# Windowed attention in steps of two heads: fixed TensorE order, scores on 64 rows a head, one division in the gate

## The chip, the cores and the metric

One Trainium2 chip, one NeuronCore of it. The number is device time in microseconds (us) of the whole program, the median of the runs. Float32 data; the large products run in float32r (operands rounded, one pass of TensorE), each operand split into a rounded part and an exact rest, and three of the four part products are added up.

## The reference

Two layers over 2048 latent tokens of width 1024 (a grid of 32 rows of 64) and 256 context tokens. Layer 0 is attention with 16 heads of 64: a latent query reads a clamped window of 8 x 16 grid positions, with a learned bias, and all 256 context keys in one softmax; context queries read the context keys. Layer 1 is a gated linear recurrence; it is not touched.

```python
s_loc = einsum('bjqhd,bkjwhd->bhjqkw', q_r, k_band) * scale + bias   # -inf outside the window
s_ctx = einsum('bjqhd,bmhd->bhjqm', q_r, k_ctx) * scale
p = softmax(concatenate([s_loc, s_ctx], -1))
o = p_loc @ v_band + p_ctx @ v_ctx
x = x + gate * ((o * silu(z)) @ w_out)                               # q, k, v, z = split(h @ w_in)
```

## The kernel before

The kernel is written in a tile framework: pools hold rotating buffers, and a scheduler, which places each instruction by its own estimate of times, sets the order of the instructions on every engine, unless `after` (L570) ties one behind another.

Layer 0 runs in three stages. The input projection writes q, k, v and z = silu(gate) to HBM (`split_out` L253, `gate_out`); the attention reads them head pair by head pair; the output projection follows. q and k are stored as two tensors each, the rounded part and the rest (`qh`, `ql`, `kh`, `kl`).

The attention (L479 on) loops over 8 pairs of heads (`hp`), and in each over 4 row groups of 8 grid rows (`g`, 512 queries) and the context queries. A row group has 4 column bands (`j`) of 128 queries, so a pair has 16 latent steps of two heads and 2 context steps. Row groups 1 and 2 read 512 window keys, 0 and 3 read 384; all read 256 context keys, so a row of scores has 768 or 640 columns. For each band and head (`a`):

- Scores (L596, L599, L615). The stationary operand is `q`, with the rounded part of a head on partitions 0 to 63 and its rest on 64 to 127; the keys stand twice, on both halves (`pair_tile` L450), so one product over 128 rows adds the products of both parts of q with `kh`, and a second one with `kl`.
- Softmax (L494 to L499). One VectorE operation adds the bias table to the scores and takes the row's minimum (the scores have their sign turned), ScalarE takes the exponential and the sum, VectorE takes the reciprocal and multiplies the row by it.
- Transposes (`turn`, L509), in pieces of 128 keys, into a bank of PSUM, copied to SBUF by ScalarE or, each sixth time, by VectorE (L513, L515).
- Weighted values (`weighted`, L522): per 128 keys one product for each head, the two heads on the two column halves of the array. Each float32 product stands as two records in the trace. The context keys are weighted for two bands at once.

At the end of a row group `gate_store` (L553) multiplies by z and stores. The bias tables come by DMA into rotating buffers (`load_table` L426: tables `tabe`, `tabi`), whose last 256 columns and masked corners GpSimd fills each time. `o_ps` has one buffer, score tiles `s` two.

Of the kernel before, what the change touches and what calls it, by code (L numbers as in the profile page):

```python
# [25 lines left out]
# scores are kept with their sign turned  # L26
# [13 lines left out]
TPS = 3  # L40
EV = "aaaaav"
TEB = 6
PB = 4
PCB = 3
# column bands whose context keys are weighted together
JB = 2
# [7 lines left out]
class Core:  # L54
# [33 lines left out]
    def ada_lanes(self, layer, g, conds, pool):  # L88
        """columns g * 512 .. + 512 of the parameters: each lane sums its rows."""
# [12 lines left out]
    def ada_sum(self, lanes, pool, psum, tag, prev):  # L102
        """TensorE sums the lanes, behind prev."""
# [22 lines left out]
    def ada_start(self, pool, psum, tag, tag2):  # L126
        """shift and scale of layer 0 from whole rows of weights: shift by lanes, scale on TensorE."""
# [49 lines left out]

    def norms(self, xts, pool, small, tag="junk"):
        """1 / rms of the rows of each tile, one column each."""
# [36 lines left out]
    def layer0_in(self):  # L216
        nc, tc, I, S = self.nc, self.tc, self.I, self.S
        with ExitStack() as st:
# [34 lines left out]
            def split_out(cg, p, t0, n, dst_h, dst_l, keys):  # L253
                oh = wk.tile([P, 512], F32R, name="oh", tag="oh")
                ol = wk.tile([P, 512], F32R, name="ol", tag="ol")
                ohv, olv, pv = oh[:, :n], ol[:, :n], p[:, :n]
                if not keys and n == 512:
                    ohv, olv = (custom(t, [[-16, 8], [P, 4], [1, 16]], 7 * 16) for t in (oh, ol))
                    pv = p.rearrange("p (r j c) -> p r j c", r=8, j=4)
                if keys:  # L260
                    nc.scalar.mul(out=ohv, in_=pv, mul=KSCALE)
                    nc.vector.scalar_tensor_tensor(olv, pv, KSCALE, ohv.bitcast(F32), ALU.mult, ALU.subtract)
                else:
                    nc.scalar.copy(out=ohv, in_=pv)
                    nc.vector.tensor_sub(olv, pv, ohv.bitcast(F32))  # L265
                r = slice(cg * P, (cg + 1) * P)
                nc.sync.dma_start(out=dst_h[r, t0:t0 + n], in_=oh[:, :n].bitcast(F32))
                nc.sync.dma_start(out=dst_l[r, t0:t0 + n], in_=ol[:, :n].bitcast(F32))

            def gate_out(cg, p, t0, n):  # L270
                sg = wk.tile([P, 512], F32, name="sg", tag="oh")
                nc.scalar.activation(sg[:, :n], p[:, :n], AF.Sigmoid)
                z = wk.tile([P, 512], F32, name="zo", tag="ol")
                nc.vector.tensor_mul(z[:, :n], p[:, :n], sg[:, :n])
                nc.sync.dma_start(out=S["z"][cg * P:(cg + 1) * P, t0:t0 + n], in_=z[:, :n])

            def q_out(pr):
                return lambda p, t0, n: split_out(pr, p, t0, n, S["qh"], S["ql"], False)

            def k_out(pr):  # L280
                return lambda p, t0, n: split_out(pr, p, t0, n, S["kh"], S["kl"], True)
# [144 lines left out]
    def load_table(self, t, head, col, g):  # L426
        """minus the bias (or a large number outside the window) for the queries of row group g,
        whose rows stand last to first."""
        nc, S = self.nc, self.S
        nk = ROWG[g][1] * 32  # L430
# [7 lines left out]
        nc.gpsimd.memset(t[:, nk:nk + CTX], 0.0)  # L438
        if g in (1, 2):
            part("ei", 0, 8, 0, 0, nr)  # L440
        elif g == 0:
            part("ei", 0, 4, 4, 0, nr)
            nc.gpsimd.memset(t[64:128, 256:nk], NEG)
            part("ef", 4, 8, 4, 0, 8)
        else:
            nc.gpsimd.memset(t[0:64, 0:128], NEG)
# [4 lines left out]
    def pair_tile(self, p, up, dn, hp, t0, n, tag, **kw):  # L451
        t = p.tile([P, 2, n], F32R, name=tag, tag=tag, **kw)
        for part, name in ((t[0:64], up), (t[64:128], dn)):
            src = self.S[name][hp * P:(hp + 1) * P, t0:t0 + n].rearrange("(a d) t -> d a t", a=2)
            self.nc.sync.dma_start(out=part.bitcast(F32), in_=src)
        return t

    def key_block(self, p, hp, i, **kw):
        r0, nr = KBLOCKS[i]
        return [self.pair_tile(p, nm, nm, hp, r0 * 64, nr * 64, f"{nm}{nr}", **kw) for nm in ("kh", "kl")]  # L460

    def first_loads(self, hp, qp, kp, cxp):
        L = {"k": {}, "q": {}, "t": {}}
        L["q"][0] = self.pair_tile(qp, "qh", "ql", hp, 0, 512, "q")
        L["k"][0] = self.key_block(kp, hp, 0)
        L["kc"] = [self.pair_tile(cxp, nm, nm, hp, SEQ, CTX, "c" + nm) for nm in ("kh", "kl")]
        return L

    def attention_ahead(self):
        """what the first scores of the first pair of heads read."""  # L470
        self.sa = ExitStack()
        ap = self.sa.enter_context(self.tc.tile_pool(name="a0", bufs=1, reuse_waits="tile", side="right"))
        self.ahead = L = self.first_loads(0, ap, ap, ap)
        for col in (0, 1):
            for a in range(2):
                t = L["t"][0, a, col] = ap.tile([P, 640], F32, name=f"tab{a}{col}")
                self.load_table(t, a, col, 0)

    def attention(self):  # L479
        nc, tc, S = self.nc, self.tc, self.S  # L480
        with ExitStack() as st:
            def pool(name, bufs, **kw):
                return st.enter_context(tc.tile_pool(name=name, bufs=bufs, reuse_waits="tile", **kw))
            vp, kp, qp, cxp = pool("av", 2), pool("ak", 2), pool("aq", 2), pool("ac", 2)
            ti, te = pool("ai", 6), pool("ae", TEB)
            wk, sm = pool("aw", PB), pool("as", 8)
            ps_s, ps_t, ps_o = pool("aps", 2, space=PSUM), pool("apt", TPS, space=PSUM), pool("apo", 4 - TPS, space=PSUM)

            self.nt = 1

            def softmax(sview, table, n):
                p = wk.tile([P, 768], F32, name="p", tag="p")
                nm = sm.tile([P, 1], F32, name="nm", tag="nm")
                nc.vector.tensor_tensor_reduce(p[:, :n], sview, table, 1.0, 3.0e38, ALU.add, ALU.min, nm)  # L494
                sums = sm.tile([P, 1], F32, name="sums", tag="sums")
# [728 lines left out]
```

## Time and profile before

| | |
|---|---|
| median of 3 runs | 3480.48 us (3478.44 to 3486.43) |
| profiled execution, span from first to last instruction | 3477.0 us |
| TensorE busy | 3333.7 us, 96% |
| VectorE, ScalarE, GpSimd busy | 1985.4, 1261.6, 759.9 us |
| attention, first score to last weighted value | about 891 to 1607 us |

The profiled execution has no time of its own beside its span; the runs' median stands 3.5 us above it, which is what lies around the first and the last instruction. A matmul's record covers its whole passage through the array, and records overlap, so the busy share of TensorE says little: what an instruction costs is read from the distance between the starts of neighbours. PEld is the loading of the stationary operand, which runs beside matmuls.

### The profile page before, as it was taken

What the parts mean: (1) busy time and instruction counts of PE and PEld (TensorE: products, weight loads), DVE (VectorE), ACT (ScalarE), POOL (GpSimd) and SP (SyncE); (2) the same over time, 40 slices, a digit from 0 to 9 for tenths busy, and PEclk for the clock granted to TensorE, in tenths of its full rate; (3) what the DMA queues carried; (4) which work ended last, traced back from release to release, by engine and by line L of the source; (5) the groups of instructions that cost most, each with busy time, mean ns of one, the idle gap of its engine ahead of it and who ended that gap; (6) DMA issues with size and microseconds to landing.
All of it is one profiled execution on the core that took longest, in us unless ns stands there. A gap on an engine that the chain in (4) does not pass through costs nothing. (4 is left out here: it accounts for less than half of the span.)

```text
span 3477.0 us, 57414 instructions
## 1 busy us (share of the span) xinstructions
PE 3333.7 (96%) x22276; PEld 2727.7 (78%) x22276; DVE 1985.4 (57%) x4315; ACT 1261.6 (36%) x2688; POOL 759.9 (22%) x787
## 2 busy tenths in 40 slices
PE   7999999999889999999999999999899999999898
PEld 5778989989667777777888888888778777887687
DVE  7674111111457666675744555555775677777876
ACT  4311110010456666664312333333443344444521
POOL 2210110010012111112322222222342222232321
PEclk9999999999989999999999999999999999999999
DMA  6665232233777778763341111111232333332542
GB/s 234 178 198 186 82 105 77 75 106 112 168 191 180 182 174 189 172 163 99 133 142 43 58 47 55 55 56 55 94 100 78 104 114 115 116 116 98 179 145 106
DMA packets 259880, 424.46 MB, mean 122 GB/s; under 512 B 34956, under 2 KB 138124, under 8 KB 259608
## 3 DMA queue, kind: packets, MB, share of 16 engines
q1 hardware_dynamic: 244824, 372.54, 37.6%
q0 software_dynamic: 14784, 48.25, 3.6%
q8 instruction: 176, 2.88, 0.4%
q14 instruction: 96, 0.79, 0.1%
HBM read 295.22 MB, written 126.96 MB: 121 GB/s over the span
## 5 line engine op out<-in xcount | busy, mean ns | idle before, releaser
L210 PE MATMUL g_ps<-h1h,g_wh 128*128 128x512 f32 x1280 | 517.1, 404 | 5.2 <-DVE qt L984 2.6
L212 PE MATMUL g_ps<-h1h,g_wl 128*128 128x512 f32 x1280 | 516.8, 404 | 0.0
L211 PE MATMUL g_ps<-h1l,g_wh 128*128 128x512 f32 x1280 | 515.3, 403 | 0.0
L210 PE MATMUL mm<-hi,wh 128*128 128x512 f32 (+1 forms) x960 | 351.1, 372 | 5.1 <-DVE ol L265 3.5
L212 PE MATMUL mm<-hi,wl 128*128 128x512 f32 (+1 forms) x960 | 353.8, 370 | 1.8 <-POOL wl L70 1.8
L211 PE MATMUL mm<-lo,wh 128*128 128x512 f32 (+1 forms) x960 | 355.3, 371 | 0.2
L210 PEld LDWEIGHTS g_ps<-h1h,g_wh 128*128 128x128 f32 x1280 | 241.9, 189 | 61.2 <-DVE qt L984 2.9
L212 PEld LDWEIGHTS g_ps<-h1h,g_wl 128*128 128x128 f32 x1280 | 241.8, 189 | 56.0
L211 PEld LDWEIGHTS g_ps<-h1l,g_wh 128*128 128x128 f32 x1280 | 241.7, 189 | 54.0
L496 ACT ACTIVATE p<-p,nm 128x768 f32<-128x768 f32 (+2 forms) x288 | 243.2, 845 | 90.5 <-DVE nm L494 87.0
L70 POOL TENSOR_TENSOR g_wl<-g_raw,g_wh 128x1024 fp32r<-128x1024 f32 x86 | 210.1, 2444 | 292.8 <-ACT g_wh L67 279.9
L509 PE MATMUL tps<-ident,p 128*128 128x128 f32 x1472 | 249.5, 288 | 2.2 <-ACT pc L513 2.0
L818 DVE COPY_PREDICATED pm<-masks,lv 128x256 f32<-128x256 int32 x192 | 85.7, 447 | 271.7 <-PE lv L804 271.5
L509 PEld LDWEIGHTS tps<-ident,p 128*128 128x128 f32 x1472 | 167.0, 144 | 66.8 <-issue 56.7
L210 PEld LDWEIGHTS mm<-hi,wh 128*128 128x128 f32 x960 | 180.2, 189 | 39.4 <-DVE ol L265 4.8
L212 PEld LDWEIGHTS mm<-hi,wl 128*128 128x128 f32 x960 | 181.4, 189 | 33.5 <-POOL wl L70 2.7
L211 PEld LDWEIGHTS mm<-lo,wh 128*128 128x128 f32 x960 | 181.5, 189 | 32.5 <-issue 1.7
L522 PE MATMUL o_ps<-pt,vb 128*64 128x128 f32 x1792 | 176.3, 291 | 25.3 <-DVE ot L562 11.6
L513 ACT COPY pt<-tps 128x512 f32<-128x512 f32 (+2 forms) x283 | 145.8, 515 | 136.5 <-PE tps L509 134.3
L816 ACT COPY km<-k 128x512 f32<-128x512 f32 x192 | 129.3, 673 | 172.0 <-PE lv L804 152.5
L70 POOL TENSOR_TENSOR wl<-wraw,wh 128x1024 fp32r<-128x1024 f32 x24 | 57.5, 2395 | 590.8 <-ACT wh L67 590.8
L761 DVE TENSOR_TENSOR k<-k,F 128x512 f32<-128x512 f32 (+1 forms) x240 | 164.8, 688 | 38.2 <-PE lv L824 33.8
(271 smaller groups left out, 7450.2 us busy)
## 6 DMA issues: line engine op xcount, KB each, us to landing
g_raw<-in_w SPq DMA_DIRECT2D x90, 512.0 KB
wraw<-in_w SPq DMA_DIRECT2D x32, 512.0 KB
adaw<-in_ada_w SPq DMA_DIRECT2D x64, 256.0 KB
vb<-s_v SPq DMA_DIRECT2D x128, 128.0 KB
kh<-s_kh SPq DMA_DIRECT2D x32, 384.0 KB
kl<-s_kl SPq DMA_DIRECT2D x32, 384.0 KB
tabi<-s_ei SPq DMA_DIRECT2D x48, 256.0 KB
s_v<-vo SPq DMA_DIRECT2D x72, 128.0 KB
```

Of the source, the lines that this page charges most:

```text
L70: e_lo.tensor_sub(lo, src, hi.bitcast(F32))
L210: nc.tensor.matmul(ps, wh(dc), hh(dc), start=dc == 0, stop=False)
L211: nc.tensor.matmul(ps, wh(dc), hl(dc), start=False, stop=False)
L212: m = nc.tensor.matmul(ps, wl(dc), hh(dc), start=False, stop=dc == n - 1)
L496: nc.scalar.activation(p[:, :n], p[:, :n], AF.Exp, bias=nm, scale=-1.0, accum_out=sums)
L509: nc.tensor.transpose(ps[:, c, :], p[:, at:at + P], self.ident)
L513: nc.scalar.copy(out=out, in_=ps[:, :n, :])
L522: last[a] = nc.tensor.matmul(o[64 * a:64 * a + 64], values(c, a), ps[a][:, c], start=last[a] is None, stop=end and c == nv - 1)
L761: nc.vector.tensor_mul(kv, kv, kf)
L816: nc.scalar.copy(out=km.rearrange("p (k h i) -> p k h i", h=2, i=b), in_=self.mixed(k2, T, b))
L818: nc.vector.copy_predicated(pm, self.masks[:, j, :].unsqueeze(1).broadcast_to([P, 4, 64]), ps)
```

## The change

The attention is written anew, as steps of both heads of a pair, and the stage before it stores q and k in one tensor each.

- The scratch tensors are `q` and `k` of shape [2, D, TOK]; a pair's tile holds head 0 on partitions 0 to 63 and head 1 on 64 to 127, and the two parts in its free dimension. One DMA stores or loads both parts. The keys are no longer held twice.
- Scores: three products a head and key part (rounded with rounded, rounded with rest, rest with rounded) over the head's own 64 rows; the product of the rests is left out. The two heads' products alternate.
- The rows of p are not divided. The sums of a row group are kept, their reciprocals are spread on a diagonal by GpSimd (`spread`), four small products with a matrix of ones bring them to the layout of `o_ps` (`rb`, in `gate`), and the gate multiplies z by them before it multiplies the output.
- Transposes of a step go to three banks (window keys of head 0, of head 1, context keys of both); ScalarE copies the first, VectorE the other two.
- All products of the attention are tied in one chain (`pin`): the scores of a step, the transposes of the step before, the weighted values of the one before that.
- Bias tables stand in fixed tiles, one set for each of row groups 0, 1 (used by 2 too) and 3; their constant parts are filled once.

```diff
-    def pair_tile(self, p, up, dn, hp, t0, n, tag, **kw):
-        t = p.tile([P, 2, n], F32R, name=tag, tag=tag, **kw)
-        for part, name in ((t[0:64], up), (t[64:128], dn)):
-            src = self.S[name][hp * P:(hp + 1) * P, t0:t0 + n].rearrange("(a d) t -> d a t", a=2)
-            self.nc.sync.dma_start(out=part.bitcast(F32), in_=src)
+    def rows_of(self, tile, name, hp, t0):
+        src = self.S[name][:, hp * P:(hp + 1) * P, t0:t0 + tile.shape[2]].rearrange("h p t -> p h t")
+        self.nc.sync.dma_start(out=tile.bitcast(F32), in_=src)
...
+    def new_tables(self, pool, g):
+        nk = ROWG[g][1] * 32
+        for col in range(3):
+            for a in range(2):
+                t = T[a, col] = pool.tile([P, nk + CTX], F32, name=f"tab{g}{a}{col}", bufs=1)
+                nc.gpsimd.memset(t[:, nk:], 0.0)
...
-                rs = sm.tile([P, 1], F32, name="ars", tag="ars")
-                nc.vector.reciprocal(rs, sums)
-                nc.vector.tensor_scalar(p[:, :n], p[:, :n], rs[:, 0:1], None, ALU.mult)
...
+            def pin(m):
+                if chain[0] is not None:
+                    self.after(m, chain[0])
+                chain[0] = m
...
+                    for at, m, kv in parts:
+                        for i, (hq, hk) in enumerate(((0, 0), (0, 1), (1, 0))):
+                            for a in range(2):
+                                r = slice(64 * a, 64 * a + 64)
+                                pin(nc.tensor.matmul(s[a][:, at:at + m], q[r, hq, j * P:(j + 1) * P], kv(r, hk), start=i == 0, stop=i == 2))
+                    for a in range(2):
+                        p = wk.tile([P, 768], F32, name="p", tag="p", bufs=5)
+                        nc.vector.tensor_tensor_reduce(p[:, :n], s[a][:, 512 - nk:768], t, 1.0, 3.0e38, ALU.add, ALU.min, nm)
+                        nc.scalar.activation(p[:, :n], p[:, :n], AF.Exp, bias=nm, scale=-1.0, accum_out=R.sums[:, a, j:j + 1])
...
+                    groups = [(a, [(a, c) for c in range(nl)]) for a in range(2) if nl]
+                    groups.append((2, [(a, nl + c) for a in range(2) for c in range(2)]))
+                    for k, what in groups:
+                        ps = ps_t.tile([P, 4, P], F32, name="tps")
+                        for i, (a, c) in enumerate(what):
+                            pin(nc.tensor.transpose(ps[:, i, :], self.p[a][:, c * P:(c + 1) * P], ident))
+                        if k == 2:
+                            nc.vector.tensor_copy(out, ps.rearrange("p (a c) q -> p a c q", a=2))
+                        elif k == 0:
+                            nc.scalar.copy(out=self.pt[:, k, :nl], in_=ps[:, :nl])
+                        else:
+                            nc.vector.tensor_copy(self.pt[:, k, :nl], ps[:, :nl])
...
+            def spread(R, steps):
+                nc.vector.reciprocal(rs[:, :, :steps], R.sums[:, :, :steps])
+                for a in range(2):
+                    for j in range(steps):
+                        nc.gpsimd.tensor_scalar(R.dg[:, a, j], ident, rs[:, a, j:j + 1], None, ALU.mult)
+            def gate(R, steps):
+                for j in range(0, steps, 2):
+                    for a in range(2):
+                        pin(nc.tensor.matmul(rb[64 * a:64 * a + 64, j:j + 2], ones, dg[:, a, j:j + 2], start=True, stop=True))
+                nc.vector.tensor_mul(z, turned[1], z)
+                nc.vector.tensor_mul(out, turned[0], z)
...
+            while True:
+                new = next(todo, None)
+                if new:
+                    new.scores()
+                if at:
+                    at.turns()
+                if before:
+                    before.weighted()
+                before, at = at, new
```

On TensorE, in a row group of 512 window keys, the order before was this (`s` scores, `kh_...` and `kl_...` key blocks of the two parts, `ckh` and `ckl` context keys, `tps` transposes, `o_ps` weighted values):

```order
L596 MATMUL s<-kh_13640,q 128x256
L596 MATMUL s<-kl_13643,q 128x256
L596 MATMUL s<-kh_14260,q 128x256
L596 MATMUL s<-kl_14263,q 128x256
L599 MATMUL s<-ckh,q 128x256
L509 MATMUL tps<-ident,p 128x128 x3
L599 MATMUL s<-ckl,q 128x256
L509 MATMUL tps<-ident,p 128x128 x2
L522 MATMUL o_ps<-pt,vb 64x128
L509 MATMUL tps<-ident,p 128x128 x4
```

The same kind of step now (`k_...` key blocks, `kc` context keys; a row of six is three products for each of two heads):

```order
L568 MATMUL s<-k_10681,q 128x256 x6
L568 MATMUL s<-k_11288,q 128x256 x6
L568 MATMUL s<-kc,q 128x256 x6
L589 MATMUL tps<-ident,p 128x128 x12
L612 MATMUL o_ps<-pt,vb 64x128 x8
L612 MATMUL o_ps<-pc,vc 64x256 x4
L568 MATMUL s<-k_11288,q 128x256 x6
L568 MATMUL s<-k_11498,q 128x256 x6
L568 MATMUL s<-kc,q 128x256 x6
L589 MATMUL tps<-ident,p 128x128 x12
```

Score products went from 12 in a step to 18, and the three kinds of work stand in whole blocks.

On VectorE, in the same kind of row group, before (the `ISA` rows are the table's addition with the minimum, and the reading of that minimum):

```order
L498 RECIPROCAL ars<-sums 128x1
L494 ISA p,nm<-s,tabi 128x768
L494 ISA nm 128x1
L499 TENSOR_SCALAR p<-p,ars 128x768
L498 RECIPROCAL ars<-sums 128x1
L499 TENSOR_SCALAR p<-p,ars 128x768
L494 ISA p,nm<-s,tabi 128x768
L494 ISA nm 128x1
L498 RECIPROCAL ars<-sums 128x1
L560 TENSOR_TENSOR ot<-o_ps,zt 128x512
L499 TENSOR_SCALAR p<-p,ars 128x768
L515 COPY pc<-tps 128x2x128
```

And now, with the gate of the row group before it behind the copies:

```order
L574 ISA p,nm<-s,tab_6971 128x768
L574 ISA nm 128x1
L574 ISA p,nm<-s,tab_6973 128x768
L574 ISA nm 128x1
L596 COPY pt<-tps 128x512
L592 COPY pc<-tps 128x4x128
L650 TENSOR_TENSOR zt<-rb,zt 128x512
L651 TENSOR_TENSOR ot<-o_ps,zt 128x512
```

The rows' multiplications are gone, two copies a step and a second operation in the gate have come.

## Rows read from the trace of the kernel before

**Rows 1.** Windows: stage before, attention, one pair, after; columns in the first row.

```profile
core 0: us, PE busy (x) PEld busy (x) DVE busy (x) ACT busy (x) POOL busy (x), PEclk, DMA share, GB/s
0.00:880.00 880.00, 851.38 (x4838) 731.21 (x4839) 293.29 (x540) 143.51 (x232) 108.78 (x71) 0.99 0.41 134
891.00:1607.00 716.00, 656.84 (x5190) 508.89 (x5189) 480.95 (x1287) 445.28 (x1041) 107.12 (x275) 0.95 0.73 173
1276.00:1357.00 81.00, 79.96 (x651) 62.00 (x651) 59.26 (x161) 54.31 (x131) 12.81 (x35) 0.99 0.78 186
```

**Rows 2.** Timeline of TensorE: start, length, instruction; scores, transposes, values, transposes.

```profile
1209.16 0.28 PE L599 MATMUL s<-ckh,q 128*128 128x256 f32 x1
1209.28 0.28 PE L599 MATMUL s<-ckl,q 128*128 128x256 f32 x1
1209.39 0.38 PE L509 MATMUL tps<-ident,p 128*128 128x128 f32 x2
1209.71 1.09 PE L522 MATMUL o_ps<-pt,vb 128*64 128x128 f32 x16
1210.73 0.66 PE L509 MATMUL tps<-ident,p 128*128 128x128 f32 x4
1211.14 0.36 PE L596 MATMUL s<-kh,q 128*128 128x256 f32 x1
```

**Rows 3.** Timeline of TensorE: scores of 384 columns, then of 256.

```profile
1178.14 0.34 PE L596 MATMUL s<-kl,q 128*128 128x384 f32 x1
1178.32 0.28 PE L599 MATMUL s<-ckh,q 128*128 128x256 f32 x1
```

**Rows 4.** Timeline of TensorE: products of one column, each with 128 stationary columns.

```profile
35.07 1.92 PE L156 MATMUL ada_tp<-one,acc 128*128 128x1 f32 x16
```

**Rows 5.** Timeline of TensorE in layer 1: float32 products over the whole array.

```profile
1918.94 0.39 PE L839 MATMUL o_ps<-t_v,pf 128*128 128x128 f32 x2
1919.17 0.39 PE L842 MATMUL o_ps<-sf,q 128*128 128x128 f32 x2
```

**Rows 6.** Groups of VectorE in the attention: count, busy us, mean ns, idle before.

```profile
L494 DVE CUSTOM_DVE_ANT_0 p<-s,tabi 128x768 f32<-128x768 f32 x128 | 121.8, 952 | 40.1 <-PE tps L509 19.8 <-PE s L599 17.6 <-DMA tabi<-s_ei 2.3
L494 DVE CUSTOM_DVE_ANT_0 p<-s,tabe 128x640 f32<-128x640 f32 x122 | 99.9, 820 | 56.2 <-DMA tabe<-s_ef 28.8 <-PE tps L509 7.0 <-PE s L599 6.4
L499 DVE TENSOR_SCALAR p<-p,ars 128x768 f32<-128x768 f32 x128 | 83.6, 653 | 3.0
L515 DVE COPY pc<-tps 128x256 f32<-128x256 f32 x86 | 36.2, 421 | 31.4 <-PE tps L509 30.8
L494 DVE DVE_READ_ACCUMULATOR2_ANT nm<- 128x1 f32 x288 | 23.8, 83 | 0.0
L560 DVE TENSOR_TENSOR ot<-o_ps,zt 128x512 f32<-128x512 f32 x32 | 22.0, 688 | 20.3 <-DMA zt<-s_z 14.1 <-PE o_ps L522 6.2
```

**Rows 7.** Group of GpSimd: its operation nearest in size to the diagonal's.

```profile
L204 POOL TENSOR_TENSOR h1l<-hf,h1h 128x256 fp32r<-128x256 f32 x16 | 12.5, 780 | 27.3 <-ACT h1h L203 27.3
```

**Rows 8.** Waits in the attention: in total us, times, longest.

```profile
PEld tps L509 <- issue: 56.7, 199, 0.8
PEld s L596 <- DVE nm L494: 35.6, 19, 6.0
```

**Rows 9.** Timeline at the attention's start: VectorE twice, then TensorE.

```profile
897.94 0.82 DVE L494 CUSTOM_DVE_ANT_0 p<-s,tab 128x640 f32<-128x640 f32 x1 [5.37 <-DMA s_z<-zo]
...
933.68 0.69 DVE L560 TENSOR_TENSOR ot<-o_ps,zt 128x512 f32<-128x512 f32 x1 [10.82 <-DMA zt<-s_z]
...
934.43 0.91 PE L522 MATMUL o_ps<-pt,vb 128*64 128x128 f32 x6 [8.74 <-DVE ot L560]
```

**Rows 10.** DMA in the attention: packets and rate; issues of one key load.

```profile
DMA packets 94628, 123.79 MB, mean 173 GB/s; under 512 B 7764, under 2 KB 60395, under 8 KB 94556
...
kh<-s_kh SPq DMA_DIRECT2D x30, 384.0 KB
```

More of the change, by code (lines that the diff above doesn't have):

```diff
@@ L39 @@
 PSB = {"mm": 3, "lv": 2, "tr": 2, "o": 1}
[L40 to L44, printed above, removed]
 JB = 2
@@ L251, in granule, with split_out @@
                 return wh, wl
[L253 to L259, printed above, removed]
+            def split_out(cg, p, t0, n, name, keys):
+                t = wk.tile([P, 2, 512], F32R, name="st", tag="st")
+                oh, ol, pv = t[:, 0, :n], t[:, 1, :n], p[:, :n]
@@ L472, in attention_ahead @@
         ap = self.sa.enter_context(self.tc.tile_pool(name="a0", bufs=1, reuse_waits="tile", side="right"))
[L473 to L477, printed above, removed]
+        self.tabs = {0: self.new_tables(ap, 0)}
+        self.ahead = self.first_loads(0, ap, ap, ap)
+        for (a, col), t in self.tabs[0].items():
+            self.load_table(t, a, col, 0)
     def attention(self):
@@ L502, in turn @@
-            def turn(p, parts):
-                at = 0
-                for out in parts:
-                    n = out.shape[1]
-                    ps = ps_t.tile([P, 4, P], F32, name="tps")
-                    for c in range(n):
-                        nc.tensor.transpose(ps[:, c, :], p[:, at:at + P], self.ident)
-                        at += P
-                    self.nt += 1
-                    if EV[self.nt % len(EV)] == "a":
-                        nc.scalar.copy(out=out, in_=ps[:, :n, :])
-                    else:
-                        nc.vector.tensor_copy(out, ps[:, :n, :])
@@ L517, in weighted @@
-            def weighted(o, last, nv, values, ps, end):
-                prev = last[:]
-                for c in range(nv):
-                    for a in range(2):
-                        last[a] = nc.tensor.matmul(o[64 * a:64 * a + 64], values(c, a), ps[a][:, c], start=last[a] is None, stop=end and c == nv - 1)
-                        if c == 0 and prev[a] is not None:
-                            self.after(last[a], prev[a])
-            pair_tile, key_block = self.pair_tile, self.key_block
+            wk, sm = pool("aw", 2), pool("as", 8)
@@ new lines, in attention @@
+            ps_s, ps_t, ps_o = pool("aps", 2, space=PSUM), pool("apt", 3, space=PSUM), pool("apo", 1, space=PSUM)
+            tabs = self.tabs
+            for g in (1, 3):
+                tabs[g] = self.new_tables(tp, g)
+            tabs[2] = tabs[1]
+            ones = tp.tile([P, 64], F32, name="ones")
+            nc.gpsimd.memset(ones, 1.0)
+            ident = self.ident
+            chain = [None]
+            def pin(m):
+                if chain[0] is not None:
+                    self.after(m, chain[0])
+                chain[0] = m
@@ new lines, in steps @@
+            def steps():
+                nxt = load_pair(0)
+                for hp in range(8):
+                    L = nxt
+                    for g in range(5):
+                        if g < 3:
+                            L["q"][g + 1] = self.rows_of(qp.tile([P, 2, 512], F32R, name="q", tag="q"), "q", hp, 512 * (g + 1))
+                            if g < 2:
+                                L["k"][g + 1] = self.key_block(kp, hp, g + 1)
+                        if g == 0:
+                            tables(hp, 1)
+                            tables(hp, 3)
+                        if g == 1:
+                            L["qc"] = self.rows_of(cxp.tile([P, 2, CTX], F32R, name="qc", tag="qc", bufs=1), "q", hp, SEQ)
+                        if g == 2 and hp < 7:
+                            nxt = load_pair(hp + 1)
+                        R = Rows(hp, g, L)
+                        for j in range(R.steps):
+                            yield Step(R, j)
@@ L623, in after @@
+            todo = steps()
+            at, before = None, None
+            while True:
[6 more added lines that the diff above has]
+                    before.weighted()
+                if not (new or at):
+                    break
+                before, at = at, new
+            self.sa.close()
     def after(self, ins, prev):
```

240 lines of the change are left out of this document (122 added, 118 removed).

## The prediction, on record before the run

> **What bounds the kernel now.** I read the windows first: in the attention, 716 us long, TensorE is busy 92% of the time, VectorE 67%, ScalarE 62%, the DMA engines 73% [rows 1]. The edit touches little else. In the 880 us before it TensorE is busy for 851 [rows 1], so a store of both parts by one DMA instead of two has nothing to shorten there; I cost it at nothing, and a few us either way if a staging tile comes free later. So the question is what TensorE's 716 us are made of. The timeline of one stretch says it by the starts of neighbours, not by lengths, since records overlap.
>
> - A score product of 256 columns takes 0.12 us (1209.16 to 1209.28) [rows 2], one of 384 takes 0.18 [rows 3].
> - A transpose takes 0.10 to 0.11 (four in 0.41) [rows 2].
> - Sixteen records of weighted values, with what follows them, take 1.02 [rows 2]. The last one starts at 1209.71 + 1.09 - 0.27, so 15 steps take 0.82: 0.055 each. A record of 256 columns I take as twice that, 0.11.
> - A change between whole-array and half-array work costs about 0.1: 0.32 for two transposes up to the first value, 0.10 above 2 x 0.11; and 1.02 - 16 x 0.055 = 0.14 on the way back. I take 0.12.
>
> A step of two heads with 768 columns has 12 scores, 12 transposes, 16 records of values and, every other step, 8 of context values: 1.44 + 1.32 + 0.88 + 0.44 = 4.08 us. With 640 columns: 4 x (0.18 + 0.12) + 10 x 0.11 + 12 x 0.055 + 0.44 = 3.40. A context step: 0.48 + 0.44 + 0.44 = 1.36. A pair of heads has 8, 8 and 2 of these: 62.6 us; eight pairs 501 us. The other 215 of the 716 us are three things. The waits list has 199 times at which the transposes' loads stand idle for nothing but the change of width (56.7 us) [rows 8]; there are as many ways back, so about 400 changes x 0.12 = 48 us. The granted clock is 0.95, that is, 5% of the stretch is lost to phases at 1.2 instead of 2.4 GHz: 36 us. The rest, 131 us, is waiting: for VectorE's minimum (35.6 us in one row) [rows 8], for the gate, for loads.
>
> **The change, part by part.**
>
> Scores. Three products a head instead of two, but on 64 rows, head 0 on the upper, head 1 on the lower. No row of this trace shows a product on half the rows. The nearest show half the columns: float32 records over the whole array start 0.11 apart (two in 0.23) [rows 5], those on column halves 0.055 [rows 2], so two halves do run beside each other. I take the same for row halves, as the two heads write different banks and alternate: 9 slots of 0.12 = 1.08 us, where 12 were 1.44; with 640 columns 0.90 instead of 1.20; context 0.36 instead of 0.48. The other end is no overlap at all: 2.16, 1.80 and 0.72. A gain beyond half is excluded, because each half still streams its 256 columns.
>
> The Trainium skill (TensorE: Matmul & The Clock Gate, Part 3, measured speedup) gives 3.07 for four row tiles, so 77% of the ideal; by it, an estimate, a step's scores would take 1.41 us instead of 1.08 and the sum below would end some 40 us later. No run here shows it.
>
> Transposes and values stay as many: 12 and 16 records. New are four `rb` products a row group, eight records of 256 columns: 0.86 / 4 = 0.22 a step.
>
> Changes of width. Whole blocks leave three in a step: row halves, whole array, column halves. Two are of the kind in rows 2; the one between row halves and whole array is in no row; its bounds are 0 and 0.14, and I take 0.12 as for the others: 0.36 a step, 18 steps, 8 pairs: 52 us instead of 48.
>
> The Trainium skill says that changing the tiling mode drains TensorE (TensorEngine Tiling, Key Properties), and this speaks against the change, as scores and transposes, which shared a mode, no longer do. The 0.10 and 0.14 of rows 2 agree with a short drain [rows 2]; by the rule the third change costs as much, and at nothing for it the sum would end 17 us earlier.
>
> So a step is 1.08 + 1.32 + 0.88 + 0.44 + 0.22 + 0.36 = 4.30 us; with 640 columns 0.90 + 1.10 + 0.66 + 0.44 + 0.22 + 0.36 = 3.68; a context step 1.82. A pair: 34.4 + 29.4 + 3.6 = 67.4; eight: 539 us.
>
> VectorE. Away go the multiplications (0.653 us a row of 768) [rows 6]. A step keeps 2 x (0.952 + 0.083), gets two copies of 512 elements from PSUM, which I put at 0.69 by the gate's operation of that size (a copy of 256 takes 0.42), and a quarter of two gate operations of 0.69: 3.80 us, against 4.30 on TensorE; with 640 columns 3.38 against 3.68. It stays under TensorE but close; ScalarE keeps its exponentials and loses copies. What hides it is the order: after the scores of a step TensorE has transposes and values for 2.2 us (2.6 with context values), and both minima, 2.07 us, fit in that before the next scores need the two score tiles. Queued behind the minima are the copies and the gate, which the values wait for one block later.
>
> GpSimd's diagonal is eight operations of 128 columns a row group; by the row of 256 columns, 0.78 [rows 7], at most 6.2 us, likely half. It starts after the last sum and is needed a whole step and two blocks later, about 7 us: hidden.
>
> Loads. The keys are no longer held twice: 2.36 MB a pair less, 18.9 of 123.8 MB [rows 10]. Fixed tables are refilled once their last reader is done, 30 us or more before the next.
>
> What waits remain of the 215 us? At least nothing: the end is 3480.5 - 716 + 539 = 3304. At most all but the changes, 167: 3471. I take 61, nearer to the lower end, from three rows: the start keeps its two waits of 5.37 and 8.74 us, since the first output gate's z still stands in the queue behind the first value and table loads [rows 9], 14; the clock's 5% of 539, 27; and 20 for the ends of groups and the drain at the end, about what the best pair (81 us at clock 0.99, 69 with its changes) [rows 1] loses each time on three pairs. The waits for the minimum and for the gate go with the order. Sum: 716 becomes 600, a gain of 116. The profiled span of 3477.0 becomes 3361; with the 3.5 us by which the runs' median stands above the span, 3364.5, rounded to 3364.
>
> **The rivals.**
>
> Row halves share the loading. A one-column product with 128 stationary columns takes 0.11 (sixteen in 1.92 less the last one's tail) [rows 4], so loading, not streaming, sets it; 18 score loads a step one after the other are 2.02 us, not 1.08; with 640 columns 12 are 1.34, not 0.90; context 0.67, not 0.36. A pair gets 11.6 us longer, eight 93: 3457. Against it: the halves in rows 2, loads included, keep up.
>
> Row halves don't overlap at all, the one that ends slower. Then the change does not do on TensorE what it says: six products where there were four. 1.08, 0.90 and 0.36 us a step more, 16.6 a pair, 132 us: 3496. It decides once more than 116 of these 132 us come, that is, if less than an eighth of the two heads' streaming overlaps. Only the lack of any row with row halves speaks for it.
>
> Loads set the pace. 104.9 MB at the 173 GB/s of before [rows 10] are 606 us; with the start's 14 they end at 3384. For it: DMA share 0.73 now, 0.78 in a quick pair, and a shorter stretch to do it in. Against it: 186 GB/s in that pair [rows 1].
>
> The chain stalls. With a fixed order every late copy or minimum holds all that follows. At 0.4 us a step, about VectorE's slack, 144 steps cost 58 us: 3422.
>
> **How the numbers follow.** My case, halves side by side and waits small, 3330 to 3400: 0.50. Loads 0.12, stalls 0.12, shared loading 0.10, no overlap 0.10; under 3330 (fewer waits still) 0.06. The predicted time is that of the first case, 3364; the range of 3312 to 3470 takes in loads, stalls and shared loading and leaves out the slower end and a part of the quick one. What can be told from no change here is 0.2%, 7 us. Faster: all but no overlap, and a little of shared loading, 0.87; the same 0.03; slower 0.10.
>
> **What would show it.** Right: the two heads' scores start within some ns of each other and nine slots take 1.1 us; a step of 768 columns takes 4.3 us; the attention ends some 600 us after its start; VectorE about 85% busy there. Wrong: starts 0.12 apart for all 18 scores; VectorE's waits for `tab` loads or z in steady pairs; TensorE idle before transposes for p, or before scores for the minimum; a clock well under 0.95; times outside the attention that differ by over 10 us.

## The result, and the profile after

The changed kernel takes 3368.0 us (median of 4 runs, 3364.2 to 3370.7), the one before 3481.1 on the same chip: a ratio of 0.967, 95% interval 0.9656 to 0.9685. The prediction said 3364. Its total is right, but it hides misses of opposite sign, and most of the runs below are about those.

The windows of the changed kernel (columns as in [rows 1]): the stage before, the attention, one steady pair in it, the stretch behind it, the rest.

```profile
0.00:888.00 888.00, 860.30 (x4898) 739.48 (x4899) 295.14 (x542) 145.17 (x234) 115.32 (x94) 0.99 0.41 134
888.00:1476.00 588.00, 564.61 (x6148) 457.84 (x6147) 442.47 (x967) 315.98 (x706) 191.81 (x327) 0.98 0.61 175
964.00:1035.00 71.00, 70.09 (x774) 56.61 (x770) 55.22 (x121) 39.23 (x88) 24.03 (x41) 1.00 0.66 186
1476.00:1495.00 19.00, 0.52 (x5) 0.19 (x2) 1.06 (x3) 5.15 (x6) 9.86 (x5) 0.63 0.34 109
1495.00:3362.00 1867.00, 1814.18 (x12192) 1478.59 (x12192) 1211.50 (x2489) 674.33 (x1418) 542.96 (x440) 0.99 0.30 97
```

The attention, 716 us in [rows 1], takes 588. In a steady pair TensorE is busy for 70.1 of 71 us at the full clock, VectorE for 55.2, the DMA engines for 0.66. But behind the attention stands a stretch of 19 us with nearly no TensorE work that the kernel before did not have.

TensorE's timeline in a steady stretch (start, length, instruction), which answers to [rows 2]; two steps follow each other, and the last row is the start of a third:

```profile
1291.57 0.99 PE L568 MATMUL s<-k,q 64*128 64x256 f32 x12
1292.40 0.51 PE L568 MATMUL s<-kc,q 64*128 64x256 f32 x6
1292.85 1.53 PE L589 MATMUL tps<-ident,p 128*128 128x128 f32 x12
1294.30 1.09 PE L612 MATMUL o_ps<-pt,vb 128*64 128x128 f32 x16
1295.33 1.00 PE L568 MATMUL s<-k,q 64*128 64x256 f32 x12
...
1299.00 1.03 PE L612 MATMUL o_ps<-pc,vc 128*64 128x256 f32 x8
1299.87 1.03 PE L639 MATMUL rb<-dg,ones 128*64 128x256 f32 x8
1300.83 1.00 PE L568 MATMUL s<-k,q 64*128 64x256 f32 x12
```

From start to start the scores take 1.28 us, twelve transposes 1.45, sixteen records of values 1.03, the context values 0.87, `rb` 0.96. Twelve score products of 256 columns take 0.83 us, 0.07 each; one over the whole array took 0.12 [rows 2]. So two heads run beside each other.

The last `rb` of two neighbouring pairs, and the stalls at the start and behind the attention (idle time and releaser in brackets), which answer to [rows 9]:

```profile
1054.86 0.60 PE L639 MATMUL rb<-dg,ones 128*64 128x256 f32 x4
...
1125.55 0.60 PE L639 MATMUL rb<-dg,ones 128*64 128x256 f32 x4
```

```profile
917.27 0.83 PE L589 MATMUL tps<-ident,p 128*128 128x128 f32 x4 [2.83 <-DVE zt L650]
...
953.44 1.33 PE L568 MATMUL s<-k,q 64*128 64x384 f32 x6 [10.70 <-DMA q<-s_q]
...
1494.81 0.79 PE L205 MATMUL y_ps<-woh,ohi 128*128 128x512 f32 x1 [18.48 <-ACT ohi L62]
```

A pair takes 70.69 us, and all six pairs between the first and the last repeat that within 0.02 us. (The last has no next pair's scores in it and takes 67.4.) Eight of 70.69 are 565.5 us; from the first score to the last `rb` it is 587.6, so 22 us are lost, all of them in the first pair, where the granted clock is low too (0.87; columns as above):

```profile
888.00:964.00 76.00, 60.48 (x612) 50.02 (x613) 42.99 (x90) 34.26 (x71) 15.40 (x26) 0.87 0.75 213
```

VectorE's groups in the attention (count, busy us, mean ns, idle before), which answer to [rows 6], and GpSimd's diagonal, to [rows 7]:

```profile
L574 DVE CUSTOM_DVE_ANT_0 p<-s,tab 128x768 f32<-128x768 f32 x128 | 117.3, 954 | 41.3 <-PE s L568 34.5 <-ACT p L575 5.2 <-DMA zt<-s_z 1.2
L592 DVE COPY pc<-tps 128x512 f32<-128x512 f32 x144 | 98.1, 681 | 0.4 <-PE tps L589 0.4
L596 DVE COPY pt<-tps 128x512 f32<-128x512 f32 x64 | 43.9, 686 | 0.3 <-PE tps L589 0.3
```

```profile
L632 POOL TENSOR_SCALAR dg<-ident,ars 128x128 f32<-128x128 f32 x288 | 168.6, 598 | 209.8 <-DVE ars L628 209.8
```

VectorE now waits for TensorE's scores, where TensorE waited for its minimum before [rows 8].

### The profile page after: what moved, and what is told of

Same layout as the page of the kernel before. It is cut to its first block, busy times and chain, and to the rows that moved or that the text cites. A ratio compares the mean times of both kernels' runs of the same rounds, so it can differ in the third digit from the quotient of the medians.

```text
span 3362.4 us, 58571 instructions
## 1 busy us (share of the span) xinstructions
PE 3239.6 (96%) x23236; PEld 2676.1 (80%) x23236; DVE 1950.2 (58%) x4000; ACT 1140.6 (34%) x2363; POOL 860.0 (26%) x866
## 5 line engine op out<-in xcount | busy, mean ns | idle before, releaser
L574 DVE CUSTOM_DVE_ANT_0 p<-s,tab 128x768 f32<-128x768 f32 (+2 forms) x288 | 230.0, 836 | 93.3 <-PE s L568 80.2
L632 POOL TENSOR_SCALAR dg<-ident,ars 128x128 f32<-128x128 f32 x288 | 168.6, 598 | 209.8 <-DVE ars L628 209.8
L589 PE MATMUL tps<-ident,p 128*128 128x128 f32 x1472 | 194.9, 280 | 2.8 <-DVE zt L650 2.8
L831 DVE TENSOR_TENSOR q<-q,F 128x512 f32<-128x512 f32 x192 | 184.2, 959 | 0.0
```

What stands on the lines that cost most here:

```text
L574: nc.vector.tensor_tensor_reduce(p[:, :n], s[a][:, 512 - nk:768], t, 1.0, 3.0e38, ALU.add, ALU.min, nm)
L589: pin(nc.tensor.transpose(ps[:, i, :], self.p[a][:, c * P:(c + 1) * P], ident))
L632: nc.gpsimd.tensor_scalar(R.dg[:, a, j], ident, rs[:, a, j:j + 1], None, ALU.mult)
L831: nc.vector.tensor_mul(qv, qv, qf)
```

## The experiments

Ratios are to the kernel before on the same chip. "Attention" runs from the first score to the last `rb` (without `rb`, the last value), "gap" from there to the first product of the output projection; both are of the profiled execution. The changed kernel stood at 587.6 and 18.9.

| run | median us | ratio, 95% interval | attention | gap |
|---|---|---|---|---|
| e5_control | 3365.3 | 0.9666 (0.9649 to 0.9682) | 587.8 | 18.7 |
| e1_heads_apart | 3379.9 | 0.9701 (0.9686 to 0.9717) | 587.2 | 18.8 |
| e8_nine_and_nine | 3425.1 | 0.9836 (0.9819 to 0.9852) | 645.5 | 18.9 |
| e4_no_chain | 3489.7 | 1.0015 (1.0006 to 1.0024) | 700.4 | 18.2 |
| e9_fourth_change | 3382.7 | 0.9723 (0.9707 to 0.9739) | 605.3 | 18.6 |
| e2_one_product | 3344.3 | 0.9594 (0.9580 to 0.9608) | 558.8 | 18.8 |
| e3_rows_divided | 3378.3 | 0.9692 (0.9676 to 0.9708) | 608.4 | 0.3 |
| e6_out_early | 3356.4 | 0.9640 (0.9623 to 0.9657) | 596.0 | 0.3 |
| e7_out_and_start | 3359.7 | 0.9647 (0.9631 to 0.9664) | 600.8 | 0.3 |
| e10_start_q3 | 3372.2 | 0.9689 (0.9675 to 0.9703) | 588.8 | 18.6 |
| e11_early_q3 | 3356.4 | 0.9647 (0.9634 to 0.9660) | 596.4 | 0.3 |
| e12_z_on_gpsimd | 3341.9 | 0.9595 (0.9580 to 0.9609) | 582.9 | 0.3 |

**Do the row halves overlap, and is it that which gains?**

> The changed kernel with one edit: in each key part the three score products of head 0 come first and then those of head 1, instead of alternating. The result is the same. My theory, that the gain comes from the two heads' row halves running side by side: nine slots a step of 768 columns become eighteen. By the starts in the changed kernel's trace (0.118 us for 256 columns, 0.17 for 384) that is 1.06 us more in such a step, 0.87 with 640 columns, 0.35 with the context queries: 16 us a pair, 129 in all, 3497 us, slower than the kernel before. Pairs of starts 3 ns apart should be seen only where one head ends and the other begins. Rival, that the gain comes from the fixed order and the shorter work of VectorE and the overlap adds little: within 20 us of 3368.

```diff
-                        for i, (hq, hk) in enumerate(((0, 0), (0, 1), (1, 0))):
-                            for a in range(2):
+                        for a in range(2):
+                            for i, (hq, hk) in enumerate(((0, 0), (0, 1), (1, 0))):
```

The attention did not move (587.2), and a pair takes 70.80 us; the median lies 14.6 us above the control's, on another chip, and in the profiled executions 17.7 of the 17.9 us between this run and the changed kernel lie behind the attention, which the edit leaves alone. In the trace the starts still come in pairs, 10 ns apart instead of 3. The order in the program was the wrong handle: TensorE began the other head's products ahead of its turn. The overlap was not taken away, so this run decides nothing between the theories; the next one takes more of it away.

> The changed kernel with all score products of head 0 in a step first (nine), then all of head 1. The result is the same. With three and three (e1_heads_apart) the starts still lay in pairs, 10 ns apart, so TensorE looked past the three of one head to the next head's. My theory, it looks past only a few: with nine and nine most starts stand alone, 0.118 us apart, and the step gets up to 1.06 us longer: 60 to 129 us more than the changed kernel, 3430 to 3497. Rival, it looks past any number, or the overlap is not where the time comes from: within 10 us of the changed kernel.

```diff
-                    for at, m, kv in parts:
-                        for i, (hq, hk) in enumerate(((0, 0), (0, 1), (1, 0))):
-                            for a in range(2):
+                    for a in range(2):
+                        for at, m, kv in parts:
+                            for i, (hq, hk) in enumerate(((0, 0), (0, 1), (1, 0))):
```

The attention grew by 57.7 us over the control, the low end of my range: 967 score products started within 20 ns of their neighbour before, 346 now. TensorE's timeline at a step with 640 columns, where the program has three `k`, three `kc` of head 0 and then the same of head 1:

```profile
1294.23 0.92 PE L568 MATMUL s<-k,q 64*128 64x384 f32 x4
1294.88 0.28 PE L568 MATMUL s<-kc,q 64*128 64x256 f32 x1
1294.99 0.33 PE L568 MATMUL s<-k,q 64*128 64x384 f32 x1
1295.00 0.40 PE L568 MATMUL s<-kc,q 64*128 64x256 f32 x2
```

Four `k` start before the first `kc`: the fourth is head 1's, out of its turn. It starts beside head 0's third of six, with three of head 0's still to come. With 768 columns, where head 0 has nine products, seven `k` start before the first `kc`, and the seventh, head 1's first, starts beside head 0's sixth; that is so in all 64 such steps:

```profile
1309.18 1.09 PE L568 MATMUL s<-k,q 64*128 64x256 f32 x7
1310.00 0.28 PE L568 MATMUL s<-kc,q 64*128 64x256 f32 x1
```

So here TensorE starts a product over three of the other head that come before it, but not over four or more. In both kinds of step these three are the products with `kc`, so the runs do not tell a count from something in that part.

> The changed kernel without the chain that ties the attention's products in one order; the scheduler sets TensorE's order. The result is the same. In the order that comes out the attention changes 740 times between row halves, whole array and column halves, where the chain leaves 422. My theory: each change costs some 0.15 us by the starts in the changed kernel's trace, so 318 more cost 48 us: 3416. Rival, the chain holds ready work up and the free order fills the holes: at most the 22 us by which the attention is longer than eight steady pairs, 3346.

```diff
             def pin(m):
-                if chain[0] is not None:
-                    self.after(m, chain[0])
-                chain[0] = m
+                pass
```

Far more than either theory: without the chain the whole change is worth nothing (1.0015). TensorE's windows and timeline there:

```profile
887.00:1587.00 700.00, 696.81 (x6144) 536.40 (x6143) 446.10 (x968) 322.75 (x706) 191.07 (x327) 0.99 0.53 147
```

```profile
1289.79 0.99 PE L566 MATMUL s<-k,q 64*128 64x256 f32 x6
1290.61 0.52 PE L566 MATMUL s<-kc,q 64*128 64x256 f32 x3
1291.06 0.43 PE L610 MATMUL o_ps<-pt,vb 128*64 128x128 f32 x2
1291.42 0.99 PE L566 MATMUL s<-k,q 64*128 64x256 f32 x6
1292.25 0.52 PE L566 MATMUL s<-kc,q 64*128 64x256 f32 x3
```

TensorE is hardly ever idle (697 of 700 us); it does the same work in a worse order. Two values stand between the heads, and six products of one head alone take 0.82 us, as long as twelve of both in the changed kernel. That is the overlap, measured: complete. My estimate of the rest: 533 fewer products start within 20 ns of another (434 instead of 967) at some 0.13 us each, 70 us, and 318 more changes of width at 0.15 (next run), 47: 117, where the attention grew by 113. The miss in my expectation is the first term: I had counted the changes and not the heads that were parted.

> The changed kernel with the transposes of the context keys moved behind the values of the step before, so that a step goes row halves, whole array, column halves, whole array. The result is the same. The attention changes between these kinds 548 times instead of 422. My theory, a change costs what the starts around it show: some 0.10 us at the first product behind it and 0.05 to 0.10 at the second, 0.15 to 0.2 in all, not the 0.12 of the prediction: 126 more cost 19 to 25 us, 3387 to 3393 where the changed kernel takes 3368. Rival, only the first start is late and the second is made up: 13 us or less. Second rival, the context copies that now come later on VectorE make TensorE wait: over 30 us, with waits of the values for pc.

(`late` takes the context keys' transposes, the call ahead of the values the others.)

```diff
...
                 if before:
                     before.weighted()
+                if at:
+                    at.turns(late=True)
```

A pair takes 73.03 us instead of 70.69 and has 16 changes more (69 instead of 53): 0.146 us each. The timeline shows a step of 3.94 us (1294.98 to 1298.92) where the changed kernel has 3.76 (1291.57 to 1295.33):

```profile
1294.98 1.01 PE L568 MATMUL s<-k,q 64*128 64x256 f32 x12
...
1296.29 1.09 PE L591 MATMUL tps<-ident,p 128*128 128x128 f32 x8
1297.31 1.09 PE L614 MATMUL o_ps<-pt,vb 128*64 128x128 f32 x16
1298.34 0.66 PE L591 MATMUL tps<-ident,p 128*128 128x128 f32 x4
1298.92 0.99 PE L568 MATMUL s<-k,q 64*128 64x256 f32 x12
```

A change costs about 0.15 us, not 0.12, just under the 0.15 to 0.2 of my theory: the attention grew by 17.7 us, where it said 19 to 25, and the median of 3382.7 lies below its 3387. The rival's 13 us are exceeded, and in the steady pairs no wait for `pc` shows.

**What stands behind TensorE?**

> The changed kernel, but of the three products of each score only the first (rounded q with rounded keys) is computed; the two with the rests are left out. My theory, TensorE's slots set the pace in every step: six of nine slots go, 0.71 us a step of 768 columns, 0.58 with 640, 0.24 with the context queries: 10.8 us a pair, 86 in all, 3282 us. VectorE, by the starts in the changed kernel's trace 3.3 us a step, would stay under TensorE's 3.75. Rival, VectorE or the waits between the engines already stand right behind TensorE: less than half of it comes, 3325 us or more, and TensorE stands idle before its scores for the minimum or before its transposes for p.

```diff
-                        for i, (hq, hk) in enumerate(((0, 0), (0, 1), (1, 0))):
+                        for i, (hq, hk) in enumerate(((0, 0),)):
...
```

The rival is nearer: the attention gets 29 us shorter, of the 86 that I forecast. TensorE's waits (total us, times, longest):

```profile
PE o_ps L612 <- DVE ot L651: 35.3, 32, 1.5
PE tps L589 <- DVE zt L650: 11.3, 3, 5.4
PE s L568 <- DMA q<-s_q: 11.3, 5, 3.6
```

But it is not VectorE's throughput: the quick pairs take 64.5 us with VectorE busy for 55. At each row group the next values wait for the gate to empty the only `o_ps`, and some pairs (69 to 76 us) wait for loads. In the changed kernel the longer scores cover the first.

> The changed kernel with the division back in the rows: a reciprocal and a multiplication of p on VectorE for each head and step, no diagonal on GpSimd, no products rb, one operation in the gate. The result is the same. My theory, VectorE becomes the bound: by starts in the changed kernel's trace it has 3.3 us a step of 768 columns and gets 2 x 0.57 + 2 x 0.16 - 0.17, so 4.6, against 4.2 on TensorE without rb; 0.16 us a step more than the 4.46 of now are 21 us, and the multiplication of head 1 comes so late before its transposes that up to 0.3 us a step of waiting (40 us) come on top: 3390 to 3430. Rival, the multiplications fit beside TensorE and only the rb products (0.96 us a row group) go: 35 us faster, 3333.

```diff
+                        rs = sm.tile([P, 1], F32, name="ars", tag="ars")
+                        nc.vector.reciprocal(rs, R.sums[:, a, j:j + 1])
+                        nc.vector.tensor_scalar(p[:, :n], p[:, :n], rs[:, 0:1], None, ALU.mult)
                         self.p.append(p)
...
-                        pin(nc.tensor.matmul(rb[64 * a:64 * a + 64, j:j + 2], ones, dg[:, a, j:j + 2], start=True, stop=True))
...
```

VectorE becomes the bound, as my theory said: it is busy for 69.8 of 71 us, and TensorE waits for its multiplication:

```profile
1276.00:1347.00 71.00, 67.02 (x729) 53.20 (x728) 69.80 (x183) 39.51 (x88) 2.91 (x5) 1.00 0.66 182
```

```profile
1296.03 1.59 PE L592 MATMUL tps<-ident,p 128*128 128x128 f32 x12 [0.31 <-DVE p L578]
```

But that the stage grew by 20.8 us (608.4), where I had worked out 21 from the steps, is luck. A steady pair takes 71.75 us instead of 70.69, so eight of them are 8.5 us longer, not 21. The last pair takes 80.2 us instead of 67.4 (to its last value): the gap behind the attention is gone, and the conversions of the next stage's first weights stand among the last pair's exponentials on ScalarE, so that TensorE waits there (`ars` is the reciprocal of their sum):

```profile
1434.13 1.09 PE L592 MATMUL tps<-ident,p 128*128 128x128 f32 x4 [4.06 <-DVE ars L577]
```

Why the gap is gone is not shown here; presumably it went with the space of `dg` (e6_out_early bears on that). With the gap gone, the total lies below my range. Net, no difference can be told between dividing in the gate and in the rows (0.9666 against 0.9692; the intervals overlap): what the gate gains in the stage it gives back behind it.

**The gap behind the attention, and the start.**

> The changed kernel itself once more, on the chip of the next three, so that they can be compared with it. By its first measurement, 0.967 of the kernel before; both theories expect 0.966 to 0.969.

It came out at 0.9666, as expected.

> The changed kernel with its buffer pools in another order: the tables of row groups 1 and 2, the key blocks and q lie last, next to where the output projection's weights go, instead of p, pt, dg and ot. The result is the same. In the changed kernel's trace TensorE stands idle for 18.5 us behind the attention, since the first projection weights wait for the store of the last ot. My theory, the weights take the place of buffers that the last gate still reads: with buffers there that are done some 10 us before the end or earlier, 12 to 18 us of the idle time go, about 3352 where the changed kernel takes 3368. Rival, the idle time is the loading of the last rows of o itself or GpSimd's backlog: no change.

```diff
-            tp = pool("at", 1)
-            vp, kp, qp, cxp = pool("av", 2), pool("ak", 2), pool("aq", 2), pool("ac", 2)
+            tp, vp, cxp = pool("at", 1), pool("av", 2), pool("ac", 2)
             wk, sm = pool("aw", 2), pool("as", 8)
+            qp, kp, t1p = pool("aq", 2), pool("ak", 2), pool("at1", 1)
...
-                tabs[g] = self.new_tables(tp, g)
+                tabs[g] = self.new_tables(t1p if g == 1 else tp, g)
```

The gap is gone (0.3), so my theory names its cause. In the changed kernel ScalarE's conversion of the first weights stood still for the store of `ot`, and each further load waited for the one before:

```profile
1479.70 1.99 ACT L62 CAST woh<-wor 128x1024 fp32r<-128x1024 f32 x2 [8.46 <-DMA s_o<-ot]
1486.89 1.04 ACT L62 CAST woh<-wor 128x1024 fp32r<-128x1024 f32 x1 [5.20 <-DMA wor<-in_w0o]
```

Only 9 of the 18 us came, below my range: the conversions now stand among the last pair's exponentials on ScalarE, and that pair takes 74.7 us instead of 67.4. TensorE's longest new wait in it is for an exponential:

```profile
1470.29 1.76 PE L589 MATMUL tps<-ident,p 128*128 128x128 f32 x7 [1.83 <-ACT p L575]
```

> As e6_out_early, and the first pair's loads in another order: the tables of row group 3 are fetched one row group later, the next pair's loads one row group later, both in the first pair alone. The result is the same. In the changed kernel's trace TensorE stands idle for 10.7 us before row group 3 of the first pair, for q that stands on SyncE's queue behind 17 loads of values and 12 of tables of the next pair, and VectorE for 5.3 us for z behind the tables. My theory, these are a matter of order on the queue: 12 to 18 us less than e6_out_early, the clock that falls behind each gap included; about 3336. Rival, the DMA engines themselves are behind at the start: the gap only moves to another load, within 4 us of e6_out_early.

```diff
...
+                        if g == (hp == 0):
                             tables(hp, 3)
...
-                        if g == 2 and hp < 7:
+                        if g == 2 + (hp == 0) and hp < 7:
```

My theory was wrong: the wait for `q` grew to 22.0 us. With two buffers `q` of row group 3 could not be fetched before row group 1 was done, and by then the next pair's values stood ahead of it on SyncE's queue again.

> The changed kernel with three buffers for q instead of two and, in the first pair, the tables of row group 3 fetched one row group later. The result is the same. Delaying the next pair's loads (e7_out_and_start) left q of row group 3 behind them on the queue, since its buffer was free late, and the gap grew to 22 us. My theory, the buffer is what puts q late: with a third one it goes ahead of the values, and the 10.7 us of that gap, the 5.3 of z and some 4 us of the slow clock behind them go: 12 to 20 us less, about 3352. Rival, what comes behind it on the queue is late instead: within 6 us of 3368.

```diff
-            vp, kp, qp, cxp = pool("av", 2), pool("ak", 2), pool("aq", 2), pool("ac", 2)
+            vp, kp, qp, cxp = pool("av", 2), pool("ak", 2), pool("aq", 3), pool("ac", 2)
...
+                        if g == (hp == 0):
                             tables(hp, 3)
```

The rival: no gain that can be told (0.9689 against 0.9666). The `q` gap is gone and the first pair takes 86.0 us instead of 96.0, but the second takes 81.9 instead of 70.7:

```profile
1003.38 1.11 PE L589 MATMUL tps<-ident,p 128*128 128x128 f32 x4 [6.82 <-DVE zt L650]
```

> e6_out_early and e10_start_q3 together. The result is the same. If the gap behind the attention and the stalls at its start are separate waits, their gains add up: by the 9 us of e6_out_early and 12 to 20 of e10_start_q3, 3338 to 3348. If the start is held by the DMA engines, no more than e6_out_early, 3356.

Both edits together give no more than the first (3356.4), the second of the two outcomes that I had named. The reason that I gave there, that the DMA engines hold the start, does not stand after the next run.

> e11_early_q3 with the loads of z issued by GpSimd instead of SyncE. The result is the same. In the trace of e10_start_q3 the q gap is gone from the first pair, but TensorE waits before transposes for the gate, and the gate for z (6.8 us before transposes in the second pair, 9.3 us of the gate for z), and the second pair takes 81.9 us instead of 70.7; in e11_early_q3 the stall in the first pair is 7.8 us. My theory, z stands behind some 30 loads on SyncE's queue and is what comes late: on another queue it is there, and 10 to 18 us of the two stalls and the slow clock behind them go: 3338 to 3346, against 3356 of e11_early_q3. Rival, the queue carries two pairs' loads in the time of one and whatever stands last on it is late: within 6 us of 3356, with the stall before k, kc or the tables of the second pair.

```diff
...
-                        nc.sync.dma_start(out=R.z[:, :R.n], in_=S["z"][R.hp * P:(R.hp + 1) * P, R.t0:R.t0 + R.n])
+                        nc.gpsimd.dma_start(out=R.z[:, :R.n], in_=S["z"][R.hp * P:(R.hp + 1) * P, R.t0:R.t0 + R.n])
```

My theory: 3341.9, the quickest of all, 0.7% below the changed kernel. The attention takes 582.9 us, 13.5 less than in e11_early_q3; the first two pairs lose 10.8 us over steady ones, where they lost 23.8 there. The windows of the start and of the second pair, and what is left there:

```profile
880.00:966.00 86.00, 83.14 (x839) 68.12 (x839) 59.46 (x131) 44.86 (x99) 28.38 (x52) 0.96 0.79 210
966.00:1042.00 76.00, 71.62 (x772) 58.14 (x770) 55.57 (x122) 39.41 (x89) 26.60 (x46) 0.98 0.70 202
```

```profile
1011.87 0.80 PE L568 MATMUL s<-k,q 64*128 64x384 f32 x6 [3.47 <-DMA q<-s_q]
```

The DMA engines were not full on average (0.79 in the first window, 0.77 in the same window of e11_early_q3); a small load stood behind some thirty large ones in one queue. What is left is a wait for another load on SyncE's queue, `q`, so the rival, which named `k`, `kc` or the tables, is right in part.

## Why the prediction was right, step by step

The mechanism was the one forecast: the two heads' scores run side by side, and the fixed order takes TensorE's long waits away. The number fits better than its terms do. The pairs came 26 us too short in it, the waits 39 us too long, and what lies outside the attention 14 us too short; that these cancel to 1.4 us of the span (3362.4 for 3361) is luck.

- **Scores side by side.** Right, and complete: nine slots of 0.118 us. The Trainium skill (TensorE: Matmul & The Clock Gate, Part 3, measured speedup) gives 3.07 for four row tiles, and by it I had estimated a loss for two halves, beside the sum; twelve products in 0.83 us against six of one head in 0.82 show none. The rivals "no overlap" and "shared loading" fall.
- **Changes of width.** Mis-sized: 0.36 us a step for three. The blocks are longer than their slots by 0.20 (scores 1.28 for 1.08), 0.13 (transposes 1.45 for 1.32) and 0.15 (values 1.03 for 0.88), 0.48 together, and `rb` takes 0.96 instead of 0.86 a row group. So a pair takes 70.7 us and not 67.4: 26 us too little over eight. That a change of tiling mode drains TensorE, as the Trainium skill says (TensorEngine Tiling, Key Properties), agrees with the 0.15 us that one more change costs in e9_fourth_change. The count before was wrong as well: the waits list gave me some 400 changes, but the trace of before goes 607 times between whole array and column halves. So the fixed order did not add changes, as my 52 us for 48 had it; it took the attention from 607 to 422.
- **Waits of 61 us.** Mis-sized the other way: 22 measured. The 27 for the clock were wrong: in every steady pair it is 1.00, with TensorE busy for about 70 of 71 us. The 20 for group ends were wrong too, and did not follow from their row either (81 less 69, on three pairs, is 36). Only the start's 14 came, as 10.7 for `q`, which I had not named, 2.8 for the gate, and the slow clock there (0.87). 565.5 + 22.1 make 587.6, where I had 539 + 61.
- **VectorE.** Under TensorE, as said, but with more room: 75% of the stage busy, not 85%. I added up records (0.954 a minimum, 0.69 a copy); their starts lie 0.88 and 0.60 apart, since the next begins before the last one's record ends. e3_rows_divided shows that the row multiplications would have made it the bound, by 1.06 us a pair.
- **GpSimd.** 0.598 us an operation, 4.8 us a row group, not half of 6.2. Hidden in steady pairs, as said.
- **Loads.** 405.7 MB in the kernel where 424.5 stood, 18.8 less, as worked out. They set no pace in the steady pairs, where TensorE is busy for 70 of 71 us: 175 GB/s in the attention at a share of 0.61, where that rival took 173 GB/s, reached at a share of 0.73, as the limit.
- **Outside the attention.** Costed at nothing, and wrong by what I had named as the sign of an error: 18.5 us of gap. I priced the fixed tables by their refills, and neither them nor `dg` as space; the next stage's weights then landed on the last gate's buffers. The other stretches came out some 5 us shorter; why is not known. All in all 12.4 us less in the attention and 13.8 more outside (3362.4 - 587.6 against 3477.0 - 716) than predicted.
- **The chain.** I gave it the waits that it ends. e4_no_chain shows that it does more: it keeps the two heads' products together, on which the overlap rests, and the changes few. The rival that the chain stalls falls: in a steady pair TensorE is idle for 0.9 us, before the first scores of the next.

What stays open: whether TensorE's look ahead ends at three products by count, and how the 10.6 us by which a steady pair exceeds its slots (60.1 us by the starts, 53 changes, so 0.20 each) divide between changes and small waits.

## What to carry to other kernels

When two half-array streams are to run beside each other, write their products next to each other and fix that order: the order, not only the layout, is the gain. Price each buffer that a change adds by who uses that space next, and look at the first instructions behind the changed stage. A stall at a stage's start is better traced along the issuing queue than to the load that came last: a delay or a third buffer for the late load only moved it, another queue for a small load took more than half of it away.

## What the runs showed of the hardware

- Products on different row halves start out of program order, over three products of the other half: with three and three in program order, starts lie in pairs 10 ns apart (e1_heads_apart); with six and six or nine and nine, the second head's first starts when three of the first head's are still to come, and not before (e8_nine_and_nine).
- A change between row halves, whole array and column halves delays the second product behind it too: into scores the first starts 0.20 us after the last value and the second 0.22 after the first, where 0.11 and 0.12 are usual (trace of the changed kernel, 1295.3 us).
